# Raw weights in slots of their own, pinned weight splitting and paired down projections in a two-layer decoder step

## The chip, the cores and the metric

The kernel runs on one NeuronCore of one Trainium2 chip. The metric is the time of one execution on the device in microseconds (us). An execution's "span" is the time from its first to its last instruction; its own time is a little longer.

## The reference, cut to what matters

The program is one inference step of a decoder with two layers for 512 new prompt tokens and 8 x 4 sample tokens, which share all weights; here they are one block of 544 token columns. Each layer has a first FFN, a mixing stage (windowed attention, a causal depthwise convolution, gates, three output projections) and a second FFN, with a layer norm after each.

```python
def swiglu(x, w_up, w_down):
    a, u = jnp.split(x @ w_up, 2, axis=-1)
    return (jax.nn.silu(a) * u) @ w_down

def decoder_layer(x, k_past, v_past, conv_past, p):
    x = layer_norm(ALPHA * x + 0.5 * swiglu(x, p['ffn1_up'], p['ffn1_down']), p['ln1_g'], p['ln1_b'])
    ...
    x = layer_norm(ALPHA * x + mix @ p['w_out'], p['ln2_g'], p['ln2_b'])
    x = layer_norm(ALPHA * x + 0.5 * swiglu(x, p['ffn2_up'], p['ffn2_down']), p['ln3_g'], p['ln3_b'])
```

All data is float32. The model width is 1024, the FFN's hidden width 2816.

## The kernel before

**Arithmetic.** Activations lie transposed: 1024 features are four tiles ("pairs") of 128 partitions x 2 x 544 tokens. A product keeps float32 accuracy on a faster matrix type by splitting each operand into a high part (a cast on ScalarE) and a low part (the difference, on VectorE) and adding three matmuls: high x high, high x low, low x high. So every weight is loaded raw by SyncE's queue, cast (`halves`, L265) and subtracted (L266) before TensorE can use it, and every activation is split the same way (`split`, L346 and L347).

**Pieces.** `plan` (L155) writes down the order of all weight pieces. `fetch` (L242) loads the next one, `prep` (L269) splits it, `W` (L315) hands it out and keeps a given number of pieces prepared ahead. A normal piece is 8 x 128 rows by 256 columns, two raw tiles of 512 KB. `unit` (L324) multiplies one piece with one half of the tokens ("hf", 272 columns each): 6 matmuls for each 128 rows.

**The FFN.** The hidden width is 11 blocks of 256 columns. In the first FFN of layer 0 each block takes an "a" and a "u" piece: `silu`, then `gated`. The other three calls, here called fast, do so for blocks 0 and 1 (`up_first`, L512, half by half) and for block 10; blocks 2 to 9 go as "s" pieces of 128 columns each, where seven products of 12 matmuls replace eight (Strassen's scheme in Winograd's form, over the column halves a and u, row halves and token halves). `combine` (L282) builds the sums of raw weights on VectorE (L290 to L293) and splits four tiles. `up_fast` (L555) runs the products in the order 1, 7, (3 of the unit before, in `finish`), 6, 4, 2, 5; between them copies out of PSUM stand on ScalarE (L564, L566, L569), additions on VectorE, a silu. I call this a block unit.

**Down projections.** Blocks are grouped in threes (`GROUPS = (3, 3, 3, 2)`). After the first block of a group the down projection of the group before runs: four pieces, each with both token halves (`down_unit`, L578), whose result is added to Y in SBUF (L581, called the eviction). The last group's down projection, with block 10 just before it, is interleaved with the layer norm in `tail` (L644) or, in the last call, `final` (L667). The norm of one half (`ln_fin`, L356) is put off into the matmuls of the next half by a clock that counts matmuls (`due`, L624); its steps give X of the next stage.

**What sets the order.** The program is written in one order, and a list scheduler with a model of the engines orders each engine's instructions from it and places the buffers. An instruction passed to `keep_in_program_order` is pinned behind the one traced before it on its engine. Before the change little is pinned. Buffers come from pools of equal slots: `pp` (39 slots of a pair's size: activations, raw weights and their halves alike), `fp` (10 small slots), PSUM `ps2` (3) and `ps1` (2). A load waits on SyncE's queue until its slot is free.

**Mix.** `mix` (L843) runs projections, attention, the sample tokens' attention and the convolution (taps on VectorE, L934; sample windows on GpSimd, L949) interleaved; the convolution's state is loaded on SyncE into small slots (L879). `kf` (last keys), `uo` and `vx` (values) have buffers of their own here.

## Time and profile before

| | us |
|---|---|
| three runs | 2704.52, 2696.23, 2702.84 |
| median | 2702.84 |
| the profiled execution | 2699.76 |
| its span | 2697.8 |
| granted TensorE clock, mean over the span | 0.975 |

The stages by TensorE's work: first FFN of layer 0 to 422 us, mix to 948, fast FFN to 1349, fast FFN to 1757, mix to 2277, fast FFN to the end at 2697.8.

How to read the profile: PE is TensorE's matmul, PEld its weight load, DVE VectorE, ACT ScalarE, POOL GpSimd, SP SyncE with the DMA queue; a "q" behind the name is the engine's sequencer. L537 is line 537 of the kernel. A row of a group reads: line, engine, operation, output<-inputs, shapes, xcount | busy us, mean ns of one | idle time before them and who ended it. A row of the timeline reads: start us, duration us, engine, line, operation, and in brackets the idle time before it. A row of waits reads: who <- for whom: us in total, times, longest. In the rows, "pa" and "pb" are PSUM tiles, "pr" pairs, "wh" and "wl" the high and low halves of weights, "f" small buffers.

### The profile page before, as it was taken

Reading aid. Unit: us, or ns where it says so; the run is one execution under the profiler, and the core shown is the slowest. Engines: PE = TensorE matmul, PEld = TensorE weight load, DVE = VectorE, ACT = ScalarE, POOL = GpSimd, SP = SyncE. Lnnn points to the kernel's source line nnn. Section 1 sums busy time; section 2 is a strip of 40 time slices with the busy share of each in tenths; the row PEclk is TensorE's granted clock in tenths of the full one; section 3 lists DMA queues with packets and bytes.
Section 4 is the critical chain, followed back from the end, with each engine's and each line's share of the span. In section 5 each row is a group of like instructions: output and inputs, shape, how many; then the busy total and the mean of one; then the engine's idle time right before and its main releaser. Section 6 shows DMA issues by size and latency. Waiting matters only on the chain.

```text
span 2697.8 us, 47547 instructions
## 1 busy us (share of the span) xinstructions
PE 2568.8 (95%) x20110; PEld 2515.7 (93%) x20110; DVE 1695.7 (63%) x2555; ACT 1115.0 (41%) x1946; POOL 269.7 (10%) x532
## 2 busy tenths in 40 slices
PE   8999999989899999999989999999898999999997
PEld 7999999978899989999989999999798999999997
DVE  4324246896985575756465756459969756756645
ACT  4222215566525253434253434245773443434331
POOL 2000001422300000000010000013232000000001
PEclk9999999999999999999999999999999999999999
DMA  6223123121332213323222323222214232232341
GB/s 203 80 90 102 53 92 97 51 75 59 81 96 71 90 52 94 90 87 114 95 85 90 88 90 118 80 77 68 67 52 106 71 99 75 63 94 83 91 141 34
DMA packets 302789, 232.16 MB, mean 86 GB/s; under 512 B 43976, under 2 KB 300180, under 8 KB 302480
## 3 DMA queue, kind: packets, MB, share of 16 engines
q1 hardware_dynamic: 298768, 220.37, 27.4%
q0 software_dynamic: 3808, 8.76, 1.0%
q8 instruction: 158, 2.59, 0.4%
q14 instruction: 55, 0.45, 0.1%
HBM read 225.69 MB, written 9.16 MB: 87 GB/s over the span
## 4 chain that ended last, share of the span: by engine, by line
PE 78%; DVE 9%; ACT 6%; DMA 3%; POOL 2%; issue 2%; SPq 0%; DVEq 0%; POOLq 0%; ACTq 0%
PE pa L337 20%; PE pa L339 20%; PE pa L338 19%; PE pa L537 8%; PE pb L537 6%; DMA raw<-in_ffn_up_dram 3%; DVE pr L934 3%; DVE wl L266 2%; POOL f L949 2%; ACT wh L265 2%; ACT pr L346 1%; PE pa L1044 1%; DVE pr L347 1%; PE pb L1073 1%; DVE raw L291 0%
## 5 line engine op out<-in xcount | busy, mean ns | idle before, releaser
L337 PE MATMUL pa<-pr,wh 128*128 128x272 f32 (+2 forms) x4800 | 1402.0, 293 | 31.7 <-DVE sm L1054 13.1
L339 PE MATMUL pa<-pr,wl 128*128 128x272 f32 (+2 forms) x4800 | 1397.1, 292 | 19.0 <-DVE wl L266 19.0
L338 PE MATMUL pa<-pr,wh 128*128 128x272 f32 (+2 forms) x4800 | 1392.4, 290 | 5.9 <-DVE pr L347 5.9
L337 PEld LDWEIGHTS pa<-pr,wh 128*128 128x128 f32 x4800 | 912.3, 190 | 39.1 <-DVE sm L1054 14.0
L339 PEld LDWEIGHTS pa<-pr,wl 128*128 128x128 f32 x4800 | 912.5, 190 | 23.1 <-DVE wl L266 21.2
L338 PEld LDWEIGHTS pa<-pr,wh 128*128 128x128 f32 x4800 | 919.1, 191 | 8.7 <-DVE pr L347 7.5
L265 ACT CAST wh<-raw 128x1024 fp32r<-128x1024 f32 (+1 forms) x424 | 413.1, 999 | 379.7 <-DMA raw<-in_ffn_up_dram 109.1
L266 DVE TENSOR_TENSOR wl<-raw,wh 128x1024 fp32r<-128x1024 f32 (+1 forms) x424 | 488.8, 1164 | 114.5 <-ACT wh L265 69.6
L934 DVE SCALAR_TENSOR_TENSOR pr<-u,cw,pr 128x512 f32<-128x512 f32 x480 | 343.9, 771 | 2.2 <-ACT pr L927 2.2
L537 PE MATMUL pa<-pr,wh 128*128 128x272 f32 x1536 | 304.5, 295 | 29.2 <-ACT f L566 21.5
L537 PEld LDWEIGHTS pa<-pr,wh 128*128 128x128 f32 x1536 | 245.6, 192 | 35.7 <-ACT f L566 25.7
L537 PE MATMUL pa<-pr,wl 128*128 128x272 f32 x768 | 225.2, 293 | 7.3 <-DVE wl L266 7.3
L581 DVE SCALAR_TENSOR_TENSOR pr<-pa,pr 128x544 f32<-128x544 f32 (+2 forms) x128 | 92.1, 722 | 182.0 <-PE pa L339 181.8
L416 POOL TENSOR_SCALAR nw<-nw 91x3 f32<-91x3 f32 (+2 forms) x16 | 6.4, 401 | 1741.3 <-DVE nw L412 1741.3
L346 ACT CAST pr<-f 128x544 fp32r<-128x544 f32 (+1 forms) x122 | 78.5, 648 | 202.9 <-DVE f L489 134.0
L537 PEld LDWEIGHTS pa<-pr,wl 128*128 128x128 f32 x768 | 147.8, 192 | 8.4 <-DVE wl L266 8.4
L537 PE MATMUL pb<-pr,wh 128*128 128x272 f32 x768 | 153.9, 292 | 0.0
L489 DVE TENSOR_TENSOR f<-pa,f 128x544 f32<-128x544 f32 (+2 forms) x40 | 28.9, 722 | 170.3 <-PE pa L339 156.3
L537 PEld LDWEIGHTS pb<-pr,wh 128*128 128x128 f32 x768 | 123.7, 192 | 0.0
L537 PE MATMUL pb<-pr,wl 128*128 128x272 f32 x384 | 111.5, 292 | 0.0
L347 DVE TENSOR_TENSOR pr<-f,pr 128x544 fp32r<-128x544 f32 (+1 forms) x122 | 87.6, 720 | 24.4 <-ACT pr L346 23.9
L949 POOL TENSOR_TENSOR f<-f,cw 128x124 f32<-128x124 f32 x128 | 97.2, 797 | 12.9 <-ACT f L888 12.6
(213 smaller groups left out, 2313.5 us busy)
## 6 DMA issues: line engine op xcount, KB each, us to landing
raw<-in_ffn_up_dram SPq DMA_DIRECT2D x174, 512.0 KB, 4.5
raw<-in_w_in_dram SPq DMA_DIRECT2D x72, 512.0 KB, 3.7
raw<-in_ffn_down_dram SPq DMA_DIRECT2D x64, 512.0 KB, 3.4
raw<-in_ffn_down_dram SPq DMA_DIRECT2D x48, 256.0 KB, 3.4
raw<-in_w_in_dram SPq DMA_DIRECT2D x64, 128.0 KB, 3.0
raw<-in_w_attn_out_dram SPq DMA_DIRECT2D x32, 256.0 KB, 4.2
raw<-in_w_conv_out_dram SPq DMA_DIRECT2D x16, 512.0 KB, 3.5
raw<-in_w_out_dram SPq DMA_DIRECT2D x16, 512.0 KB, 3.5
```

The lines of the kernel that those rows point to most:

```text
L265: ins = self.nc.scalar.copy(wh, t)
L266: self.nc.vector.tensor_tensor(wl, t, wh.bitcast(F32), op=ALU.subtract)
L337: self.nc.tensor.matmul(o, lhsT=wh, rhs=h, start=k == 0, stop=False)
L338: self.nc.tensor.matmul(o, lhsT=wh, rhs=lo, start=False, stop=False)
L339: self.nc.tensor.matmul(o, lhsT=wl, rhs=h, start=False, stop=k == kk - 1)
L346: pin(self.nc.scalar.copy(hi, src))
L347: pin(self.nc.vector.tensor_tensor(lo, src, hi.bitcast(F32), op=ALU.subtract))
L489: nc.vector.tensor_tensor(sa, ps, sa, op=ALU.mult)
L537: mm = lambda a, b, first=False, last=False: nc.tensor.matmul(o, lhsT=a, rhs=b, start=first, stop=last, skip_group_check=True)
L581: nc.vector.scalar_tensor_tensor(Y[p][:, :, hs], ps, 0.5, Y[p][:, :, hs], op0=ALU.mult, op1=ALU.add)
L934: self.last["cw"] = nc.vector.scalar_tensor_tensor(cc[:, m, 0:SEQ], u[:, m, k:k + SEQ], cw[:, 8 * k + c:8 * k + c + 1], cc[:, m, 0:SEQ], o ...
L949: nc.gpsimd.tensor_tensor(pr[:, 4 * b:4 * b + 4, :], win, wv.unsqueeze(1).to_broadcast([128, DS, KC]), op=ALU.mult)
```

## The change

- Raw weights get a pool of their own, `wp`, five slots; the shared pool shrinks from 39 to 37.
- In the fast calls, `steps` cuts the splitting of a piece into steps, each with a cost for ScalarE and VectorE and the slots it takes. `fill`, called at the end of each product and down unit, emits steps as long as the accounts `ta` and `td` stay within 0.4 us of TensorE's `tp` and slots (`room`) are left. Every ScalarE and VectorE instruction of this part is pinned. `V` hands out a piece and emits its missing steps at once if there are any.
- The weight sums are rebuilt in place of the raw tile, with as many operations as before. With "hi" for a cast and "lo" for a low half, the eight steps of a block piece are: hi a and S3 = a11-a21; a21 += a22; hi z (of S3) and lo a; hi u and a11 = a21-a11; a12 -= a11; hi s (the raw a tile, rewritten) and lo z; lo u; lo s.
- The seven products of a unit run in the order 1, 7, 6, 2, 5, 4, 3, and none is left for the next unit; its gate (`rest`) is emitted ahead of the next unit.
- Down projections go by two blocks (`GROUPF = (2, 2, 2, 2, 2, 1)`), in pairs of pieces between block units (`fast_order`); block 10's a piece, with its first half, comes ahead of the down projection of group 4, outside the planned steps (`P`, which pins the casts and prepares two pieces ahead), and only block 10 is left for the last group.
- `kf`, `uo` and the sample values move to small slots, the prompt values to a pair slot; the constant `c_sel` is loaded per layer into a small slot.

```diff
+GROUPF = (2, 2, 2, 2, 2, 1)
-LA, LAU, LAV, LAS, TAP, LAG, FPB = 2, 3, 2, 2, 1.2, 0.0, 10
+LA, LAU, LAV, TAP, LAG, FPB, WPB = 2, 3, 2, 1.2, 0.0, 10, 5
-PPB = 39
+PPB = 37
+ROOM = 11
+SLACK = 0.4
+        self.wp = pool("wp", WPB)
...
+    def fast_order():
+        o = [("a", 0), ("u", 0), ("a", 1), ("u", 1)]
+        o += [("dn", 0, p, hf) for hf in range(2) for p in range(2)]
+        s = lambda j, m: ("s", 2 * j + m)
+        d = lambda g, p: [("dn", g, p, hf) for hf in range(2)]
+        o += [s(2, 0), *d(0, 2), s(2, 1), *d(0, 3), s(3, 0), s(3, 1)]
+        for g in range(1, 4):
+            j = 2 * g + 2
+            o += [s(j, 0), *d(g, 0), *d(g, 1), s(j, 1), *d(g, 2), *d(g, 3), s(j + 1, 0), s(j + 1, 1)]
+        o += [("a", 10), *d(4, 0), *d(4, 1), *d(4, 2), *d(4, 3), ("u", 10)]
+        return o + [("dn", 5, p, 0) for p in range(4)]
...
-            t = self.pp.tile([128, n, 256] if kk else [128, 8, 128], F32, tag="pair", name=self.nm("raw"))
+            t = self.wp.tile([128, n, 256] if kk else [128, 8, 128], F32, tag="raw", name=self.nm("raw"))
...
+    def steps(self, key, kk, raw):
...
+        if kk:
+            for k, t in enumerate(raw):
+                w = t.shape[1] / 4
+                out.append((1.0 * w, 0, 2, lambda k=k, t=t: hi(f"d{k}", t)))
+                out.append((0, 1.2 * w, 0, lambda k=k, t=t: lo(f"d{k}", t)))
...
+        out = [(1.05, 0.7, 2, s1),
+               (0, 0.7, 0, lambda: pin(v.tensor_tensor(a21, a21, a22, op=ALU.add))),
+               (0.6, 1.2, 0, s3),
+               (1.05, 0.7, 2, s4),
+               (0, 0.7, 0, lambda: sub(a12, a12, a11)),
+               (1.05, 0.7, 2, s6),
+               (0, 1.2, 0, lambda: lo("u", Lu)),
+               (0, 1.2, 0, lambda: lo("s", La))]
...
+    def more(self):
+        n = len({c[0] for c in self.todo})
+        while n < 3 and self.loaded < self.stop:
+            got = self.fetch()
+            out, done = self.steps(*got)
...
+    def fill(self):
+        self.more()
+        end = self.tp + SLACK
+        self.ta, self.td = max(self.ta, self.tp - 3), max(self.td, self.tp - 3)
+        while self.todo:
+            _, ca, cd, room, _, _ = self.todo[0]
+            if self.ta + ca > end or self.td + cd > end or room > self.room:
+                break
+            self.step()
+
+    def V(self, *key):
+        self.more()
+        while not self.ready:
+            self.step()
...
+    def P(self, *key):
+        self.ahead(2)
+        return self.W(*key, la=1)
...
+            self.tp += 1.5
+            self.room += room
+            self.fill()
...
             product(1, b1, w, True)
-            nc.scalar.copy(A, b1)
+            pin(act.copy(A, b1))
             product(7, E, w, True)
-            nc.scalar.copy(pu[:, 1], E)
-            finish()
+            pin(act.copy(pu[:, 1], E))
             product(6, A, w)
...
+            product(3, A, w, room=2)
+            pin(act.activation(sa[:, 1], A, AF.Silu))
...
+            def rest():
+                pin(v.tensor_tensor(sa, sa, pu, op=ALU.mult))
+                self.split(hh[:, m].rearrange("p (h n) -> p h n", h=2), hl[:, m].rearrange("p (h n) -> p h n", h=2),
+                           sa, pin)
...
+        def middle():
+            self.stop = self.pi + len(self.ffn_order(l, f)) - 14
+            self.room = ROOM
+            self.tp, self.ta, self.td = 0.0, 0.0, 4.0
...
+                    w = self.V(l, f, "s", k[0])[0]
...
+                    if rest:
+                        rest()
+                    rest = up_fast(j // 2, w, hs[j], m)
...
+            rest()
+
+        if self.is_fast(l, f):
+            gl, jl = len(GROUPF) - 1, 10
+            up_first()
+            Y += self.scaled(Y0)
+            self.mark(l, f)
+            middle()
+            wa = self.P(l, f, "a", 10)
+            if last:
+                self.cut = FB[FK[1][0]][0]
+            sa0 = silu(wa, 0)
+            down(gl - 1, self.P)
...
-        kf = self.cp.tile([128, 2, NT - CUT], F32, tag="kf", name=self.nm("kf"))
+        kf = self.f1([128, 2, NT - CUT])
-        uo = self.cp.tile([128, 8, KC - 1 + NS], F32, tag="uo", name=self.nm("uo"))
+        uo = self.f1([128, 8, KC - 1 + NS])
-        vx = self.cp.tile([128, 5, NKV, HD], F32, tag="vx", name=self.nm("vx"))
+        vp = self.att([128, 4, NKV, HD])
+        vs = self.f1([NS, NKV, HD])
```

More of the change, by code (lines that the diff above doesn't have):

```diff
@@ L270, in prep @@
         key, kk, raw = got or self.fetch()
-        if not kk:
-            self.ready.append((key, self.combine(*raw), kk))
-            return
+        assert kk
         ms = []
@@ L280, in prep, with hi, lo @@
         self.ready.append((key, ms, kk))
-    def combine(self, La, Lu):
-        v = self.nc.vector
-        Ls = self.pp.tile([128, 2, 4, 128], F32, tag="pair", name=self.nm("ls"))
-        L4 = self.f1([128, 4, 128])
+    def steps(self, key, kk, raw):
+        pin = self.tc.keep_in_program_order
+        v, act = self.nc.vector, self.nc.scalar
+        new = lambda shape, n: self.pp.tile(shape, F32R, tag="pair", name=self.nm(n))
+        sub = lambda o, a, b: pin(v.tensor_tensor(o, a, b, op=ALU.subtract))
+        low = lambda o, t, h: sub(o, t, h.bitcast(F32))
+        box = {}
+        out = []
+        def hi(n, t):
+            shape = list(t.shape)
+            small = shape[1] * shape[2] <= 512 and n == "z"
+            mk = (lambda: self.f1(shape, F32R)) if small else (lambda: new(shape, "w" + n))
+            box[n] = mk(), mk()
+            pin(act.copy(box[n][0], t))
+        def lo(n, t):
+            low(box[n][1], t, box[n][0])
+        if kk:
[3 more added lines that the diff above has]
+                out.append((0, 1.2 * w, 0, lambda k=k, t=t: lo(f"d{k}", t)))
+            return out, lambda: self.ready.append((key, [box[f"d{k}"] for k in range(len(raw))], kk))
+        La, Lu = raw
@@ L296, in combine, with s1 @@
[L296 to L301 removed]
+        S3 = self.f1([128, 4, 128])
+        def s1():
+            hi("a", La)
+            sub(S3, a11, a21)
@@ new lines, in done @@
+        def done():
+            both = lambda t, cut: tuple(cut(x) for x in t)
+            a, s, u = box["a"], box["s"], box["u"]
+            self.ready.append((key, {
+                1: both(a, lambda x: blk(x, 0)), 2: both(a, lambda x: blk(x, 1)), 7: box["z"],
+                6: both(s, lambda x: blk(x, 0)), 3: both(s, lambda x: blk(x, 1)),
+                5: both(u, lambda x: blk(x, 0)), 4: both(u, lambda x: blk(x, 1))}, kk))
+        return out, done
+    def more(self):
[3 more added lines that the diff above has]
+            out, done = self.steps(*got)
+            for i, c in enumerate(out):
+                self.todo.append((got[0], *c, done if i == len(out) - 1 else None))
+            n += 1
@@ new lines, in step @@
+    def step(self):
+        _, ca, cd, room, fn, done = self.todo.popleft()
+        self.ta += ca
+        self.td += cd
+        self.room -= room
+        fn()
+        if done:
+            done()
+        self.more()
[8 more added lines that the diff above has]
+            self.step()
@@ L588, in down @@
             del H[g]
-        for g, n in enumerate(GROUPS):
-            if g == 0:
-                up_first()
-                Y += self.scaled(Y0) if Y0 else self.residual(X)
-                if f == "ffn1":
-                    if l == 0:
-                        self.setup2()
-                    self.setup_layer(l)
-            if g == 1 and f == "ffn1":
-                self.shift_caches(l)
-            for i in range(2 if g == 0 else 0, n - (g == 3)):
-                up(g, i)
-                if i == 0 and g > 0:
-                    down(g - 1)
@@ new lines, in ffn @@
+        if self.is_fast(l, f):
+            gl, jl = len(GROUPF) - 1, 10
[8 more added lines that the diff above has]
+            down(gl - 1, self.P)
+        else:
+            gl, jl, sa0 = len(GROUPS) - 1, 10, None
+            for g, n in enumerate(GROUPS):
+                if g == 0:
+                    up_first()
+                    Y += self.residual(X)
+                    self.mark(l, f)
+                if g == 1:
+                    self.shift_caches(l)
+                for i in range(2 if g == 0 else 0, n - (g == 3)):
+                    up(g, i)
+                    if i == 0 and g > 0:
+                        down(g - 1)
+            wa = self.W(l, f, "a", 10)
@@ L608, in ffn @@
+        wu = self.P(l, f, "u", 10) if self.is_fast(l, f) else self.W(l, f, "u", 10, la=1)
+        h = new_h(gl)
         ws = []
         def pre(hf):
-            sa = silu(wa, hf)
+            sa = silu(wa, hf) if hf or sa0 is None else sa0
             if hf == 0:
                 self.ahead(A2)
-                ws.extend(self.W(l, f, "dn", 3, p, la=1) for p in range(4))
+                ws.extend(self.W(l, f, "dn", gl, p, la=1) for p in range(4))
             gated(wu, h, hf, sa)
@@ L819, in setup_layer @@
         ps = self.p1()
-        nc.tensor.matmul(ps[:, :4], lhsT=self.sel, rhs=sk4[:4], start=True, stop=True)
+        sel = self.f1([4, 128])
+        nc.gpsimd.dma_start(sel, a["c_sel"])
+        nc.tensor.matmul(ps[:, :4], lhsT=sel, rhs=sk4[:4], start=True, stop=True)
         nc.vector.tensor_copy(nsks, ps[:, :4])
```

136 lines of the change are left out of this document (78 added, 58 removed).

## The prediction

> **What bounds the kernel now.** I read the page first, then busy time by stage, the waits, and the chain.
>
> ```profile
> span 2697.8 us, 47547 instructions
> ...
> PE 2568.8 (95%) x20110; PEld 2515.7 (93%) x20110; DVE 1695.7 (63%) x2555; ACT 1115.0 (41%) x1946; POOL 269.7 (10%) x532
> ```
>
> TensorE is the bound. The diff adds and removes no matmul: the same pieces are multiplied in another order. So everything it can win or lose is time in which TensorE stands or runs slowly. The profiled execution took 2699.76 us, of which 2697.8 are the span; the median of the three runs, 2702.84, lies 3.1 above it. I make the sum against 2699.76 and put the forecast on the median, with those 3.1 added.
>
> How fast can TensorE go? The chain has runs of unhindered products:
>
> ```profile
> 1103.30 3.03 PE pa L537 x24
> 1106.33 3.00 PE pb L537 x24
> ```
>
> 48 matmuls in 6.03 us: 0.1257 us each, so a product of 12 takes 1.51 and a down unit of 24 takes 3.02. With that pitch the stages can be weighed. Columns: stretch, length, PE busy (instructions), PEld, DVE, ACT, POOL, granted clock, DMA share, GB/s.
>
> ```profile
> 422.00:948.00 526.00, 499.14 (x3916) 479.37 (x3915) 391.63 (x663) 258.86 (x515) 104.45 (x192) 0.96 0.27 77
> 1002.30:1300.90 298.60, 286.12 (x2226) 283.58 (x2225) 184.96 (x244) 114.55 (x186) 0.00 (x0) 0.98 0.32 96
> 1409.60:1708.00 298.40, 286.91 (x2228) 284.12 (x2229) 184.05 (x246) 113.59 (x185) 0.00 (x0) 0.98 0.33 96
> 2330.10:2627.80 297.70, 284.70 (x2225) 281.94 (x2224) 184.71 (x244) 114.30 (x186) 1.20 (x2) 0.99 0.33 99
> ```
>
> The last three are the block units of the three fast FFN calls. At 0.1257 their matmuls need 279.8, 280.1 and 279.7 us, so 18.8, 18.3 and 18.0 us are lost: 55.1 in all. That is the most the rewritten part can win, 2% of the span. The first row is a mix stage; the change touches it only through its buffers. Where in the block units is the loss?
>
> ```profile
> 1002.30:1022.40 20.10, 14.62 (x78) 13.63 (x77) 17.26 (x22) 8.83 (x13) 0.00 (x0) 0.75 0.19 53
> 1022.40:1250.00 227.60, 220.60 (x1744) 219.05 (x1744) 146.12 (x196) 92.49 (x155) 0.00 (x0) 1.00 0.31 91
> 1250.00:1300.90 50.90, 50.90 (x408) 50.90 (x407) 21.58 (x28) 13.23 (x19) 0.00 (x0) 1.00 0.42 135
> 1409.60:1446.40 36.80, 32.33 (x215) 31.09 (x216) 27.85 (x40) 15.95 (x26) 0.00 (x0) 0.81 0.21 58
> 2330.10:2367.00 36.90, 31.39 (x222) 30.16 (x220) 28.94 (x38) 16.99 (x28) 0.00 (x0) 0.91 0.21 59
> ```
>
> The start of each call (rows 1, 4, 5) loses 20.1-9.8 = 10.3, 36.8-27.0 = 9.8 and 36.9-27.9 = 9.0: 29.1. The steady part (row 2) loses 227.6-219.2 = 8.4; by difference the other two calls lose 8.5 and 9.0, so 26.0. The end (row 3: 408 matmuls need 51.3) loses nothing. These are the three terms to follow.
>
> **The start.** Its loss is a wait and what it does to the clock: first the waiting matmul, then the clock.
>
> ```profile
> 1005.79 0.59 PE L537 MATMUL pa<-pr,wl 128*128 128x272 f32 x1 [2.90 <-DVE wl L266]
> ```
>
> ```profile
> 1005.20:1012.00 6.80, 5.75 (x24) 5.43 (x25) 5.71 (x8) 3.84 (x5) 0.00 (x0) 0.50 0.00 0
> 1018.90:1022.30 3.40, 3.40 (x17) 3.40 (x16) 2.50 (x4) 0.19 (x1) 0.00 (x0) 0.51 0.02 5
> ```
>
> After 2.90 us of waiting the granted clock is 0.50 for 6.8 us (lost: half, 3.4); a later stall costs another 3.4 us at 0.51 (lost 1.7). I call these a long and a short spell. [...]
>
> What VectorE did just before shows the sizes: a gate's product, two subtractions of weights, a low half.
>
> ```profile
> 1002.55 0.72 DVE L489 TENSOR_TENSOR f<-pa,f 128x544 f32<-128x544 f32 x1 [4.08 <-PE pa L339]
> 1003.19 0.68 DVE L290 TENSOR_TENSOR ls<-raw,raw 128x512 f32<-128x512 f32 x1
> 1003.91 0.69 DVE L291 TENSOR_TENSOR raw<-raw 128x512 f32<-128x512 f32 x1
> 1004.52 1.22 DVE L266 TENSOR_TENSOR wl<-raw,wh 128x1024 fp32r<-128x1024 f32 x1
> ```
>
> And ScalarE, from a stretch that the steady part needs again: silu, casts of weights, cast of the hidden value, copies out of PSUM.
>
> ```profile
> 1119.02 0.40 ACT L551 ACTIVATE f<-pb 128x272 f32<-128x272 f32 x1 [1.08 <-PE pb L537]
> 1119.31 1.04 ACT L265 CAST wh<-ls 128x1024 fp32r<-128x1024 f32 x1
> 1120.25 0.62 ACT L265 CAST f<-f 128x512 fp32r<-128x512 f32 x1
> 1120.77 1.05 ACT L265 CAST wh<-raw 128x1024 fp32r<-128x1024 f32 x1
> 1121.72 0.64 ACT L346 CAST pr<-f 128x544 fp32r<-128x544 f32 x1
> 1122.26 0.39 ACT L566 COPY f<-pa 128x272 f32<-128x272 f32 x1
> 1122.54 0.40 ACT L569 COPY f<-pb 128x272 f32<-128x272 f32 x1
> 1122.82 0.41 ACT L564 COPY pb<-pa 128x272 f32<-128x272 f32 x1
> ```
>
> After the change the first work is a down unit. Its casts are early, but its low half is pinned on VectorE behind the last gate of the opening blocks: product 0.72, cast of the hidden value 0.64 on ScalarE, its low half, as wide as the product, 0.72, then the weight's low half 1.22. That is 3.3 us after TensorE has finished; two matmuls run before the low half is needed, so 3.1 are idle, as long as the 2.90 of before, and I give it the same 3.4 of clock. The splits of the first block piece are pinned behind the eviction of the fourth down unit: 0.72 for a tile of that width, then one addition 0.69 and the low half 1.22, less the two free matmuls 2.4; then two subtractions and a half-size low half (0.68+0.69+0.68) behind product 1 and two matmuls (1.76): 0.3; then two low halves (2.44) behind one product (1.51): 0.9. With a short spell, 1.7, the start is 3.1+3.4+2.4+0.3+0.9+1.7 = 11.8, three times 35.4 against 29.1: **+6**. The second down piece's low half is pinned behind the first unit's eviction; TensorE, whose order is free, can run the first piece's second half meanwhile, and if it doesn't, 0.72+1.22 = 1.9 more stand open. In the second call the layer's constants are traced in between, and I take the same. Bounds: without any slow clock 6.7 each, 20.1, or -9; with long spells for both stalls and the 1.9, 15.4 each, 46.2, or +17.
>
> **The steady part.** In the eight rows above is the stall of today, which recurs every two block units: L566, a copy that empties PSUM for the next product, stands behind four casts, and TensorE waits until it is done. The pinned steps cure this inside a unit: they are set between the products by an account kept in the code, in which no step may end more than 0.4 us after the product it is set behind, and each copy has a product of 1.51 as its cover. But where two block units follow each other without a down unit, the written order is: cast of a later weight 1.05 (it takes the slot that product 3 frees, so it starts only then, and the silu and all of ScalarE queue behind it), in the worse case its low half on VectorE 1.22, then the gate's product 0.72, its cast 0.64, and only then the copy that product 6 of the next unit waits for, 0.41: 4.0 us against products 1 and 7, 3.0. About 1.0 us at six such places a call is 6. TensorE's own order is not pinned and may put a product of a later unit there, so 0 is the other bound. I take 5, nearer to today's 8.4, which has the same freedom: 3 x 5 against 26.0, **-11** (-8 to -26).
>
> The counts cost nothing by themselves. A block piece is split with four additions or subtractions, four casts and four low halves, as before. The down groups of two blocks add 16 evictions a call, 3 x 16 x 0.72 = 34.6 us of VectorE, hidden while VectorE works 185 of 298.6 us; without that cover they would cost that much. Loads:
>
> ```profile
> raw<-in_ffn_up_dram SPq DMA_DIRECT2D x174, 512.0 KB, 4.5
> ```
>
> Five raw slots hold two block pieces and a half; the next piece is fetched a unit (10.6 us) ahead of a landing of 4.5, so ScalarE's pinned casts should not meet a missing load. The extra load of c_sel on GpSimd's queue is needed by no one before mix.
>
> **The end.** This is new. Piece ("a", 10) leaves the planned steps; its cast is pinned on ScalarE behind the last block's rest. From the last product: silu 0.40, product 0.72, cast of h 0.64, cast of the weight 1.05, its low half 1.22, less two matmuls: 3.8 us idle, with nothing else for TensorE, where row 3 above lost none. It is longer than the 2.90, so a short spell or a long one: 1.7 to 3.4, I take 2.5. 6.3, three times: **+19** (11 with no slow clock, 22 with long spells).
>
> **The tail.** The last down group shrinks from two blocks to one, and half of block 10 moves ahead. Between the last eviction of the first half and its normalised X, today:
>
> ```profile
> 1325.31 0.72 DVE L581 SCALAR_TENSOR_TENSOR pr<-pa,pr 128x544 f32<-128x544 f32 x1 [1.51 <-PE pa L339]
> ...
> 1354.51 0.72 DVE L347 TENSOR_TENSOR pr<-pr,pr 128x544 fp32r<-128x544 f32 x1
> ```
>
> ```profile
> 1355.29 0.60 PE L338 MATMUL pa<-pr,wh 128*128 128x272 f32 x1 [2.01 <-DVE pr L347]
> ```
>
> 29.2 us of normalisation have 192 matmuls, 24.1 us, beside them, and TensorE waits at the end. After the change 144 matmuls, 18.1, are left. If the normalisation gains nothing, 6 more us are open; if its steps, which are set by TensorE's progress, move up as much, 0. I take 3, at two such ends: **+6**. The final call has no stage behind it.
>
> **Mix.** SyncE waits for buffers:
>
> ```profile
> SPq L162 <- PE pa L339: 658.3, 100, 29.2
> ...
> SPq L879 <- DVE pr L952: 34.8, 2, 17.8
> ```
>
> ```profile
> PE pa L339 <- DVE wl L266: 19.0, 10, 5.9
> ```
>
> Raw weights no longer wait for a slot of the shared pool (first row), so part of the 19.0 us in which low halves come late should go, with the slow clock behind it. Against that, three long-lived tiles (kf, uo, the sample values) move into the ten small buffers, for which the state loads of L879 wait already, and these stand in the same queue ahead of weights. I take **-8** for both stages together; bounds -28 (19.0 plus three spells of 3.4 of clock) and +20 (the longest wait of L879, 17.8, once more in one stage).
>
> Sum: 6-11+19+6-8 = +12; 2699.8+12 = 2711.8 on the profiled execution, 2715 on the median.
>
> **Rivals.** (1) *Faster: slots were the disease.* If late raw weights cause most waits, mix gives back 28 instead of 8 and the steady part 26 instead of 11: 12-20-15 = -23, 2680. For it: the 658.3 us of slot waits on SyncE. Against it: today's repeating gap ends with ScalarE's order (the eight rows), not with a load. It decides from 20 us beyond what I took, 12 to undo the sum and 8 to be measurable. 0.35 for all that ends faster. [...] (2) *Nothing measurable:* the stalls at the ends are half as dear (no slow clock, normalisation moves up): 12-7-6 = -1, 2702. 0.20. (3) *Much slower:* the small buffers choke mix, +20 instead of -8: 2743. For it: L879. Against it: those tiles can be loaded late. 0.12.
>
> **The numbers.** A measurement of this kernel can tell 0.3%, 8 us. My forecast, +8 to +30 with its middle at 2715, has 0.33 and its own range 2711 to 2733; with rival 3, slower has 0.45, same 0.20, faster 0.35. The range reaches from a little beyond rival 1 to rival 3: 2676 to 2742.
>
> **What would show it.** Right: the start of each call still at half clock, about 12 us lost; a wait of about 3.8 us on L265/L266 where block 10 begins, absent today; copies no longer behind casts inside a unit; the wait on the split X longer by about 3. Wrong: a start without a wait of 3 us, or block 10 beginning at once (then faster); or mix, 526 us today, moved by more than 10 us either way.

## The result, and the profile after

| | before | after |
|---|---|---|
| runs, us | 2704.52, 2696.23, 2702.84, 2700.74 | 2779.95, 2781.07, 2782.53 |
| median of these, us | 2701.79 | 2781.07 |
| the profiled execution, us | 2699.76 | 2779.95 |
| granted TensorE clock, mean | 0.975 | 0.968 |

The changed kernel is slower: 1.0297 times the time before, 95% interval 1.0275 to 1.0318. A fourth execution after the change, 3590.61 us at a granted clock of 0.648, is left out of the ratio. The forecast was 2715, in a range of 2676 to 2742: slower was right, the size was not.

The page of the changed kernel, its head and the row of busy time:

```profile
span 2778.2 us, 47552 instructions
...
PE 2603.3 (94%) x20110; PEld 2540.0 (91%) x20110; DVE 1725.8 (62%) x2591; ACT 1126.9 (41%) x1938; POOL 301.7 (11%) x533
```

The matmuls are as many as before (x20110). So I count the 80.4 us by which the span grew (2778.2 less 2697.8) as time in which TensorE stands or runs at a lower granted clock: 0.968 in the mean where it was 0.975, and 0.50 to 0.51 in stretches that the last section shows. To place them I cut each execution at the first matmul of the layer norm that ends each stage and count, in each stretch, its length less 0.1257 us for each matmul in it; I call this the loss. A loss by counts is safer than the length of a stage, because the mark may move past some matmuls. Columns: stretch, length, PE busy (matmuls), PEld, DVE, ACT, POOL, granted clock, DMA share, GB/s. The stages are mix, fast FFN, fast FFN, mix, fast FFN. Before:

```profile
404.50:930.30 525.80, 498.94 (x3915) 479.17 (x3914) 394.02 (x664) 263.45 (x520) 106.25 (x193) 0.96 0.26 76
930.30:1329.90 399.60, 384.30 (x3002) 380.72 (x3002) 245.55 (x333) 158.53 (x249) 6.63 (x22) 0.99 0.29 88
1329.90:1737.00 407.10, 389.70 (x3026) 385.90 (x3026) 250.64 (x342) 160.05 (x252) 16.95 (x42) 0.97 0.31 94
1737.00:2257.90 520.90, 497.33 (x3914) 477.10 (x3913) 393.93 (x664) 263.10 (x520) 107.66 (x192) 0.97 0.26 77
2257.90:2697.80 439.90, 406.99 (x3196) 402.82 (x3194) 267.41 (x371) 164.72 (x261) 15.94 (x46) 0.98 0.28 85
```

After:

```profile
404.90:917.90 513.00, 492.65 (x3894) 472.54 (x3893) 393.97 (x663) 262.30 (x520) 125.89 (x193) 0.98 0.28 80
917.90:1351.80 433.90, 403.46 (x3073) 397.24 (x3072) 255.59 (x346) 160.79 (x245) 4.27 (x22) 0.97 0.26 78
1351.80:1787.50 435.70, 399.92 (x3026) 393.45 (x3026) 259.94 (x354) 162.75 (x248) 18.30 (x43) 0.96 0.28 88
1787.50:2302.10 514.60, 490.89 (x3844) 469.48 (x3843) 394.47 (x663) 268.04 (x524) 123.87 (x192) 0.97 0.27 80
2302.10:2778.20 476.10, 424.96 (x3216) 417.55 (x3214) 277.67 (x384) 167.62 (x257) 13.06 (x46) 0.95 0.24 73
```

Losses before: 33.7, 22.2, 26.7, 28.9, 38.2. After: 23.5, 47.6, 55.3, 31.4, 71.8. The two mix stages lose 62.6 before and 54.9 after, 7.7 less; the three fast calls 87.1 and 174.8, 87.7 more. Inside the first of these calls, in order: the start of the block units, the steady part, the beginning of block 10, the tail.

```profile
975.00:1020.00 45.00, 39.58 (x286) 38.79 (x285) 24.16 (x33) 15.60 (x19) 0.00 (x0) 0.91 0.11 33
1020.00:1290.00 270.00, 253.67 (x1963) 250.64 (x1962) 167.47 (x222) 104.31 (x165) 0.00 (x0) 0.98 0.29 89
1290.00:1305.30 15.30, 11.99 (x73) 11.45 (x73) 5.83 (x7) 4.67 (x7) 0.00 (x0) 0.78 0.24 74
1305.30:1420.00 114.70, 103.95 (x801) 102.07 (x800) 69.27 (x101) 42.95 (x62) 18.30 (x43) 0.97 0.31 100
```

Losses: 9.0, 23.3, 6.1, 14.0. The steady part, which lost 8.4 before, is the largest. It loses at three places that come back every 72 to 74 us, that is once in four block units and eight down units. Here are two of them, in rows of the timeline (start, duration, engine, line, operation, idle time before). First, ScalarE, VectorE and TensorE around a copy out of PSUM:

```profile
1138.44 0.40 ACT L678 ACTIVATE f<-pb 128x272 f32<-128x272 f32 x1 [0.37 <-PE pb L647]
1140.46 0.64 ACT L462 CAST pr<-f 128x544 fp32r<-128x544 f32 x1 [1.62 <-DVE f L684]
1141.02 0.38 ACT L666 COPY pb<-pa 128x272 f32<-128x272 f32 x1
```

```profile
1138.38 0.68 DVE L312 TENSOR_TENSOR raw<-raw,raw 128x512 f32<-128x512 f32 x1
1139.10 0.69 DVE L312 TENSOR_TENSOR raw<-raw 128x512 f32<-128x512 f32 x1
1139.71 0.72 DVE L684 TENSOR_TENSOR f<-f,f 128x544 f32<-128x544 f32 x1
```

```profile
1141.45 1.77 PE L647 MATMUL pa<-pr,f 128*128 128x272 f32 x12 [1.63 <-ACT pb L666]
```

The silu of one unit is done at 1138.84. VectorE has two subtractions of weights pinned ahead of the gate's product (L684); ScalarE waits 1.62 us for that product with its cast (L462), and the next unit's copy (L666) is pinned behind this cast. TensorE waits for the copy. The matmuls that wait are those of product 7: their weights "f" are the split of S3, the only weights in a small buffer. The rows show that the copy was held by the cast and not by its input: TensorE had finished product 1, the copy's input, by 1139.8, and the copy starts only at 1141.02, when the cast (1140.46, 0.64 us) is all but done.

Second, an eviction behind the same gate chain:

```profile
1165.48 1.22 DVE L312 TENSOR_TENSOR wu<-raw,wu 128x1024 fp32r<-128x1024 f32 x1
1166.62 1.22 DVE L312 TENSOR_TENSOR ws<-raw,ws 128x1024 fp32r<-128x1024 f32 x1
1167.75 0.72 DVE L684 TENSOR_TENSOR f<-f,f 128x544 f32<-128x544 f32 x1
1169.18 0.73 DVE L463 TENSOR_TENSOR pr<-f,pr 128x544 fp32r<-128x544 f32 x1 [0.71 <-ACT pr L462]
1169.83 1.35 DVE L694 SCALAR_TENSOR_TENSOR pr<-pa,pr 128x544 f32<-128x544 f32 x2
```

```profile
1159.49 0.28 PE L455 MATMUL pa<-pr,wd 128*128 128x272 f32 x1
...
1168.63 0.29 PE L455 MATMUL pa<-pr,wd 128*128 128x272 f32 x1
1170.69 0.36 PE L453 MATMUL pa<-pr,wd 128*128 128x272 f32 x1 [1.77 <-DVE pr L694]
```

The two evictions (L694, x2) are ten us late. The scheduler, free to order TensorE's work, had put two down units between the products of the block unit, and TensorE finished them by 1159.8 (first row); a third followed the unit's last product and took the last of the three tiles of its PSUM pool, and at 1168.9 there was none for the fourth. But VectorE's evictions are pinned behind the unit's gate chain, which needs the last product (done at 1165.9), and behind two low halves of weights; the chain's own low half waited 0.71 us more for ScalarE. The third place is the single matmul that is written ahead of product 1 (L663, here called the dummy): it waits 1.1 us for a cast of weights on ScalarE and stands in the list of waits at run 5, below. Behind some of these waits TensorE also runs at half clock (0.50 and 0.51) for 3.4 us; the last section has the rows.

At the start, and where block 10 begins:

```profile
998.08 0.55 PE L453 MATMUL pa<-pr,wd 128*128 128x272 f32 x1 [2.26 <-ACT wd L322]
1014.36 0.39 PE L647 MATMUL pa<-pr,wa 128*128 128x272 f32 x1 [2.30 <-DVE wa L312]
1298.85 0.60 PE L453 MATMUL pa<-pr,wh 128*128 128x272 f32 x1 [2.87 <-ACT wh L291]
```

### The profile page after: what moved, and what is told of

It is laid out like the page before. It is cut to its first block, busy times and chain, and to the rows that moved or that the text cites. A ratio compares the mean times of both kernels' runs of the same rounds, so it can differ in the third digit from the quotient of the medians.

```text
span 2778.2 us, 47552 instructions
## 1 busy us (share of the span) xinstructions
PE 2603.3 (94%) x20110; PEld 2540.0 (91%) x20110; DVE 1725.8 (62%) x2591; ACT 1126.9 (41%) x1938; POOL 301.7 (11%) x533
## 4 chain that ended last, share of the span: by engine, by line
PE 71%; DVE 14%; POOL 7%; ACT 4%; issue 3%; DMA 1%; DVEq 0%; POOLq 0%; ACTq 0%
PE pa L455 17%; PE pa L453 17%; PE pa L454 17%; PE pa L647 9%; PE pb L647 7%; POOL f L1110 3%; DVE pr L1095 3%; POOL pr L1114 2%; DVE wl L292 1%; ACT pr L462 1%; DVE raw L312 1%; DVE pr L463 1%; DVE f L684 1%; DVE ws L312 1%; DVE pr L694 1%
## 5 line engine op out<-in xcount | busy, mean ns | idle before, releaser
L453 PE MATMUL pa<-pr,wh 128*128 128x272 f32 (+1 forms) x4032 | 1181.2, 295 | 39.2 <-ACT pr L462 22.5
L455 PE MATMUL pa<-pr,wl 128*128 128x272 f32 (+1 forms) x4032 | 1178.1, 293 | 18.1 <-DVE wl L292 17.7
L454 PE MATMUL pa<-pr,wh 128*128 128x272 f32 (+1 forms) x4032 | 1177.2, 293 | 4.6 <-DVE pr L463 3.9
L453 PEld LDWEIGHTS pa<-pr,wh 128*128 128x128 f32 x4032 | 769.5, 192 | 48.1 <-ACT pr L462 25.7
L455 PEld LDWEIGHTS pa<-pr,wl 128*128 128x128 f32 x4032 | 771.3, 192 | 20.4 <-DVE wl L292 20.1
L454 PEld LDWEIGHTS pa<-pr,wh 128*128 128x128 f32 x4032 | 776.4, 193 | 10.0 <-DVE pr L463 8.0
L292 DVE TENSOR_TENSOR wl<-raw,wh 128x1024 fp32r<-128x1024 f32 (+1 forms) x268 | 309.5, 1182 | 89.5 <-ACT wh L291 58.8
L453 PE MATMUL pa<-pr,wd 128*128 128x272 f32 x768 | 226.4, 297 | 21.8 <-DVE pr L694 16.7
L454 PE MATMUL pa<-pr,wd 128*128 128x272 f32 x768 | 225.5, 294 | 0.0
L455 PE MATMUL pa<-pr,wd 128*128 128x272 f32 x768 | 224.6, 296 | 0.5 <-DVE wd L312 0.5
L694 DVE SCALAR_TENSOR_TENSOR pr<-pa,pr 128x544 f32<-128x544 f32 (+2 forms) x176 | 124.3, 720 | 126.7 <-PE pa L455 126.7
L462 ACT CAST pr<-f 128x544 fp32r<-128x544 f32 (+1 forms) x124 | 79.7, 646 | 290.0 <-DVE f L605 166.5
L453 PEld LDWEIGHTS pa<-pr,wd 128*128 128x128 f32 x768 | 149.3, 195 | 25.5 <-issue 20.6
L647 PE MATMUL pa<-pr,wa 128*128 128x272 f32 x1152 | 164.6, 292 | 6.9 <-DVE wa L312 6.9
L647 PE MATMUL pb<-pr,ws 128*128 128x272 f32 x1152 | 165.0, 294 | 0.0
L647 PEld LDWEIGHTS pb<-pr,ws 128*128 128x128 f32 x1152 | 155.5, 195 | 0.0
L454 PEld LDWEIGHTS pa<-pr,wd 128*128 128x128 f32 x768 | 150.2, 196 | 0.0
L455 PEld LDWEIGHTS pa<-pr,wd 128*128 128x128 f32 x768 | 148.7, 195 | 1.0 <-DVE wd L312 1.0
```

Source lines behind the costliest of these rows:

```text
L292: self.nc.vector.tensor_tensor(wl, t, wh.bitcast(F32), op=ALU.subtract)
L453: self.nc.tensor.matmul(o, lhsT=wh, rhs=h, start=k == 0, stop=False)
L454: self.nc.tensor.matmul(o, lhsT=wh, rhs=lo, start=False, stop=False)
L455: self.nc.tensor.matmul(o, lhsT=wl, rhs=h, start=False, stop=k == kk - 1)
L462: pin(self.nc.scalar.copy(hi, src))
L647: mm = lambda a, b, first=False, last=False: nc.tensor.matmul(o, lhsT=a, rhs=b, start=first, stop=last, skip_group_check=True)
```

## The experiments

The losses of every run, by the same count, in the two mix stages and the three fast calls. Ratios are to the kernel before, measured beside each run.

| run | median us | ratio, 95% | mix | fast calls |
|---|---|---|---|---|
| before | 2701.79 | | 62.6 | 87.1 |
| after | 2781.07 | 1.0297 (1.0275 to 1.0318) | 54.9 | 174.8 |
| 1 before, storage of the change | 2653.73 | 0.9841 (0.9824 to 0.9857) | 47.8 | 54.8 |
| 2 before, 41 common slots | 2690.45 | 0.9970 (0.9958 to 0.9982) | 64.6 | 75.6 |
| 3 before, four raw slots | 2654.28 | 0.9838 (0.9823 to 0.9852) | 46.8 | 55.8 |
| 4 after, no pins in the middle | 2686.61 | 0.9958 (0.9943 to 0.9973) | 56.2 | 78.0 |
| 5 after, evictions free | 2734.89 | 1.0140 (1.0124 to 1.0155) | 55.5 | 127.0 |
| 6 after, weight steps free | 2753.44 | 1.0209 (1.0192 to 1.0226) | 56.6 | 145.2 |
| 7 after, only weight steps pinned | 2706.99 | 1.0028 (1.0016 to 1.0041) | 58.1 | 101.3 |
| 8 after, block 10 by steps | 2753.93 | 1.0209 (1.0194 to 1.0224) | 56.3 | 149.4 |
| 9 runs 4 and 8 together | 2673.82 | 0.9907 (0.9892 to 0.9922) | 56.1 | 66.9 |
| 10 run 9, last group of two | 2639.59 | 0.9784 (0.9769 to 0.9798) | 51.0 | 37.3 |
| 11 after, order mended, pinned | 2763.38 | 1.0244 (1.0228 to 1.0259) | 54.1 | 159.1 |
| 12 run 10, order mended, pinned | 2724.57 | 1.0101 (1.0086 to 1.0116) | 47.5 | 129.4 |

The theory after the result: the storage gives time back, the written and pinned order of ScalarE and VectorE takes more than that, and the ends of a call add to it. The rival: the order of the units itself costs the time, pinned or not.

### Storage: runs 1 to 3

Run 1 is the kernel before with the change's buffers alone.

```diff
-PPB = 39
+PPB = 37
...
+        self.wp = pool("wp", WPB)
...
-            t = self.pp.tile([128, n, 256] if kk else [128, 8, 128], F32, tag="pair", name=self.nm("raw"))
+            t = self.wp.tile([128, n, 256] if kk else [128, 8, 128], F32, tag="raw", name=self.nm("raw"))
...
```

> The kernel before with only the storage of the change: raw weights in five slots of their own, 37 pair slots instead of 39, the four small tensors moved to the shared small slots; order, casts and block units as before. Theory (the gain of 18 to 19 us in the two mix stages comes from the raw slots, since prefetch there no longer waits for a pair slot; the loss of some 98 us lies in the new order and its pins): about 2684 us, faster than before by 15 to 20 us, the mix stages about 515 us each between the marks of the layer norms. Rival (the mix gain comes from the new order in the calls on either side): 2702 us within 5, mix stages 526 and 521 us as before. Second rival (two fewer pair slots starve the old order of the block units): slower than 2710 us.

Measured: 2653.73, more than expected. Mix gives back 14.8, and the fast calls, of which the expectation had said nothing, give back 32.3. Is it the number of slots or their being apart? Run 2 has run 1's moved small tensors and 41 common slots; run 3 is run 1 with four raw slots, so 41 in all.

```diff
-PPB = 39
+PPB = 41
...
```

> The kernel before with the small tensors moved as in the change, and the freed storage put into more of the common slots (41 instead of 39) in place of five slots for raw weights alone. Theory (what the raw slots give is that a raw transfer never waits for a slot of long life to come free): 2690 to 2702 us, well above the 2654 of the kernel with slots of its own for raw weights. Rival (what counts is the number of slots): within 8 us of 2654.

```diff
-LA, LAU, LAV, LAS, TAP, LAG, FPB, WPB = 2, 3, 2, 2, 1.2, 0.0, 10, 5
+LA, LAU, LAV, LAS, TAP, LAG, FPB, WPB = 2, 3, 2, 2, 1.2, 0.0, 10, 4
```

> The kernel before with the small tensors moved and four slots for raw weights beside 37 pair slots, 41 in all: as many as the run that kept 41 common slots (2690 us), one fewer than the run with five raw slots (2654). Theory (raw weights need slots that no long-lived tile takes, not more slots): 2655 to 2670 us. Rival (the number of slots decides): 2685 to 2695.

Measured: 2690.45 and 2654.28. Equal in number, 36 us apart: raw weights need slots that no long-lived tile can take. The waits of TensorE for the copy of L566, the repeating gap of the prediction, show what that buys. Before, and in run 2:

```profile
PE pa L537 <- ACT f L566: 21.5, 19, 1.9
```

```profile
PE pa L537 <- ACT f L566: 12.0, 13, 1.9
```

In runs 1 and 3 no matmul waits for this copy. The waits of ScalarE's casts for a transfer fall in the same order, before, in run 2, in run 3:

```profile
ACT wh L265 <- DMA raw<-in_ffn_up_dram: 109.1, 38, 7.1
```

```profile
ACT wh L265 <- DMA raw<-in_ffn_up_dram: 74.9, 32, 6.7
```

```profile
ACT wh L266 <- DMA raw<-in_ffn_up_dram: 42.8, 30, 4.5
```

So late loads and late copies go together. The step between is argued and not shown: a cast that waits for its transfer would hold up the copies behind it on ScalarE, but in the eight rows of the prediction the casts ahead of the copy stand back to back, and none of them waits for a transfer. The scheduler's order on ScalarE also differs between the kernel before and run 1, and no run separates that from the loads. Run 1's fast call between 1014.2 and the layer norm has no stop of TensorE over 0.5 us.

### Pins: runs 4 to 7

Run 4 takes every pin of the middle (the part of a fast call from the first down unit to the last block unit) away and leaves the written order.

```diff
     def steps(self, key, kk, raw):
-        pin = self.tc.keep_in_program_order
+        pin = lambda i: i
...
     def ffn(self, l, f, XYT, vg, vb, last):
-        pin = self.tc.keep_in_program_order
+        pin = lambda i: i
```

> The changed kernel with none of the pins of the middle: steps, copies, adds, gate chain and evictions are written in the same order but the scheduler may place them. Theory (the loss comes from instructions held in the written order on ScalarE and VectorE, not from the order of units): 2710 to 2740 us. Rival (the loss comes from the order of the units, with down pairs between block units and one block in the last group): 2775 to 2790 us. Second rival (the pins keep casts from going ahead of copies, and without them copies wait longer as in the kernel before): slower than 2800 us.

Measured: 2686.61, faster than the theory's 2710 to 2740. The loss of the fast calls falls by 96.8 to 78.0, and the steady part is clean:

```profile
1020.00:1260.00 240.00, 239.51 (x1909) 239.07 (x1908) 159.00 (x213) 98.56 (x159) 0.00 (x0) 1.00 0.32 95
```

1909 matmuls need 240.0 us: nothing is lost, with the same units, the same 16 extra evictions a call and the same casts. The rival, the order of the units as written, falls. TensorE's own order changed with the pins, since the scheduler sets it: in run 4 product 1 of two units, at 1111.38 and 1113.01, stands ahead of product 7 of the first. So the run prices the pins together with the order that they leave to TensorE. Which pins? Run 5 frees the evictions alone, run 6 the weight steps alone, run 7 all but the weight steps.

```diff
-                    down_unit(D[g, p], g, p, hf, pin)
+                    down_unit(D[g, p], g, p, hf)
```

> The changed kernel with one thing undone: the evictions of the down units in the middle of a fast call are no longer pinned in the order written, so they need not stand behind the gate chain on VectorE. Theory (the evictions behind the gate chain hold the PSUM slots of the down units and stop TensorE for 1.9 us once per four block units, some ten times over the three calls): 2782 falls by 15 to 22 us, to 2760 to 2767, and the idle time of L453 and L647 that ends on L694 shrinks to a few us. Rival (the stall is the copies behind casts on ScalarE, and an unpinned eviction only lets the next wait appear there): 2776 to 2784, with the idle time on L666 growing by what L694 loses.

Measured: a gain of 46 us, twice what the theory gave. The waits of TensorE of the changed kernel that stand in a steady part, and what run 5 leaves of them:

```profile
PE pa L647 <- ACT pb L666: 23.6, 15, 2.2
...
PE pa L453 <- DVE pr L694: 16.7, 14, 1.8
...
PE pb L663 <- ACT wa L322: 10.1, 9, 1.1
```

```profile
PE pa L647 <- ACT pb L666: 23.6, 15, 2.2
```

Two of the three recurring waits go, not one: the dummy's wait on the cast is gone with the eviction's. Time at half clock goes with them. The steady part of the first call now runs at a granted clock of 1.00 and loses 8.9 us, where it lost 23.3 at 0.98:

```profile
1020.00:1275.00 255.00, 247.83 (x1958) 246.47 (x1958) 167.50 (x222) 103.76 (x165) 0.00 (x0) 1.00 0.32 94
```

Of these 14.4 us, the waits that are gone make 9.2 (5.8 for evictions, 3.4 for the cast) and two spells of half clock 3.4.

```diff
     def steps(self, key, kk, raw):
-        pin = self.tc.keep_in_program_order
+        pin = lambda i: i
```

> The changed kernel with only the casts of the weight steps unpinned; copies, adds, gate chain and evictions of the block units and down units keep their written order among themselves. Theory (two separate causes: evictions held behind the gate chain, and copies held behind casts): the copy and dummy waits on ScalarE go (30 to 45 us), the waits on the eviction stay (about 20 us): 2735 to 2755 us. Rival (one cause, the evictions behind the chain; casts matter little): 2770 us or more. Second rival (all of the loss comes from where the casts stand): 2690 to 2710 us.

Measured: 2753, inside the first theory's numbers but not by its mechanism. The copy still waits:

```profile
PE pa L647 <- ACT pb L666: 21.8, 15, 2.2
PE pa L453 <- DVE pr L694: 19.3, 21, 1.9
```

Run 6 frees the casts of the steps and also their subtractions and low halves, so the copies are held mainly by the gate chain written ahead of them, and by no weight step. At 1133.88, for example, the gate's product follows the silu with no subtraction ahead of it, and the copy still makes TensorE wait 1.33 us.

```diff
     def ffn(self, l, f, XYT, vg, vb, last):
-        pin = self.tc.keep_in_program_order
+        pin = lambda i: i
```

> The changed kernel with the pins on the weight steps alone: copies, adds, gate chains and evictions of the middle are free, so the casts keep their order among themselves but not against the block units. Theory (a queue loses when both kinds stand in one written order; an order among the casts alone costs nothing, since they are in order anyway): 2685 to 2695 us, as with no pins at all (2687). Rival (each kind of pin has its own price, and the casts' share is the 28 us that freeing them gave): 2705 to 2730 us.

Measured: 2707, the rival's number: against run 4 the pins of the weight steps cost 20 us. They cost most of it at the start of a call. In the first fast call 45 us hold 294 matmuls from 975 to 1020, 8.0 lost, where run 4 has 358 and loses none, and the whole call loses 9.7 more than in run 4; from 1020 to 1260 only 2.4 are lost (1890 matmuls). The start waits as in the changed kernel, 2.26 us for a cast (L322) at 1002.56 and 2.30 us for a low half (L312) at 1018.89; the 2.30 stands in all three calls. Run 4 has neither wait in this call. The prices do not add up: 46 and 28 alone against 94 together, where the weight steps' share is 20 with all else free. A wait that one edit removes can uncover another: the waits for an eviction (L694), 14 in the changed kernel, are 21 in run 6.

### The ends of a call: runs 8 to 10

Run 8: block 10's first piece goes through the planned steps.

```diff
-            self.stop = self.pi + len(self.ffn_order(l, f)) - 14
+            self.stop = self.pi + len(self.ffn_order(l, f)) - 13
...
-            wa = self.P(l, f, "a", 10)
+            wa = self.V(l, f, "a", 10)
```

> The changed kernel with the first half of block 10 taken through the planned steps instead of being cast in one go behind the last block unit's rest. Theory (that cast leaves TensorE idle for 3.3 us and at half clock for 6.8 us, in each of three calls, some 6 us each): 2764 to 2768 us, and the idle time on L291 and L292 of piece a 10 gone. Rival (the same wait moves to the next piece or step, since ScalarE and VectorE are late there anyway): 2778 to 2784 us.

Measured: a gain of 27 us, more than the 17.3 that the beginning of block 10 loses in the changed kernel (6.1, 5.5 and 5.7 in the three calls). Where the other 10 come from, this run alone does not settle: its order of matmuls differs from the changed kernel's in the tail as well.

Run 9 is runs 4 and 8 together.

> The two edits that have paid together: no pins in the middle of a fast call, and the first half of block 10 taken through the planned steps. Theory (the two losses are separate: held order in the middle, and the cast of block 10 at its end): 2687 falls by three calls of 3.7 us idle and 3.4 us at half clock, some 21 us, to 2661 to 2669. Rival (without pins the scheduler already places that cast as early as it can, so nothing is left to gain): 2682 to 2690.

Measured: 2673.8, 13 under run 4: between theory and rival. Of the wait at the beginning of block 10, 1.6 to 1.7 us are left in each call.

Run 10 turns the groups of the down projection round, one block first and two last. It also puts block 10's two pieces next to each other, and the down projection of group 4 between the block units of block 9.

```diff
-GROUPF = (2, 2, 2, 2, 2, 1)
+GROUPF = (1, 2, 2, 2, 2, 2)
...
-            j = 2 * g + 2
+            j = 2 * g + 1
...
-        o += [("a", 10), *d(4, 0), *d(4, 1), *d(4, 2), *d(4, 3), ("u", 10)]
+        o += [s(9, 0), *d(4, 0), *d(4, 1), s(9, 1), *d(4, 2), *d(4, 3), ("a", 10), ("u", 10)]
```

> The kernel of the run before (no pins, block 10 through the steps) with the groups of the down projection turned round: the first group has one block and the last has two, as many pieces and evictions as before. Theory (in the tail a last group of one block makes each down unit wait for the split that has just been made, 1.5 to 3.4 us at five places, since no other block's products can go first; two blocks hide it): 8 to 15 us faster than the run before it, 2648 to 2658 if that one gives 2665, and the idle time on the hidden split line falls under 10 us. Rival (the waits in the tail are those of the layer norm's chain on GpSimd and stay): within 4 us of the run before it.

Measured: a gain of 34 us, more than twice the theory, and the fastest kernel of the study: 2639.59, 0.9784 of the time before. In the final call, run 9 waits for the split of a hidden value just made:

```profile
2643.81 0.58 PE L453 MATMUL pa<-pr,wh 128*128 128x256 f32 x1 [3.36 <-ACT pr L462]
```

Run 10 has no such wait there. With two blocks in the last group there are products of the other block that can run first and cover silu, gate and split. The losses of the three fast calls fall from 10.6, 18.9 and 37.4 to 5.8, 8.8 and 22.6.

### Pins in a better order: runs 11 and 12

Run 11 keeps every pin of the changed kernel and moves three things in the written order: `then` is written ahead of a product's weight steps, `fill=False` leaves the steps out, and `first` is the copy and behind it the gate chain of the unit before.

```diff
-            product(1, b1, w, True)
-            pin(act.copy(A, b1))
+            product(1, b1, w, True, then=first)
...
-            product(3, A, w, room=2)
-            pin(act.activation(sa[:, 1], A, AF.Silu))
+            product(3, A, w, room=2, then=lambda: pin(act.activation(sa[:, 1], A, AF.Silu)), fill=False)
```

> The changed kernel with every pin kept and three places of the written order changed: a product's copy, add or silu is written ahead of the weight steps that follow it; no weight steps are written between a block unit's last silu and its gate chain; and where two block units follow each other, the gate chain is written behind the next unit's first copy. Theory (the pins cost because of the order that was written, two subtractions ahead of the gate and the hidden split ahead of the copy, not as such): the 1.6 us waits on the copy, the 1.8 us waits on the eviction and the 1.1 us waits of the dummy go, some 55 us: 2720 to 2740 us. Rival (any fixed order of these queues loses, since durations and landings differ from the planned account): 2765 us or more. Second rival (the steps only slide to the next product and push the copy there): 2745 to 2765.

The same 74 us of the steady part, one period of the changed kernel, in it and in run 11:

```profile
1169.00:1243.00 74.00, 67.72 (x532) 66.91 (x532) 46.62 (x63) 29.59 (x47) 0.00 (x0) 1.00 0.31 92
```

```profile
1169.00:1243.00 74.00, 71.63 (x554) 69.65 (x553) 47.88 (x64) 30.58 (x48) 0.00 (x0) 1.00 0.29 86
```

74 - 66.9 = 7.1 lost become 74 - 69.6 = 4.4. The waits of 1.6 and 1.8 us are gone and more, shorter ones have come, of up to 0.5 us, such as this:

```profile
1170.96 0.36 PE L453 MATMUL pa<-pr,wd 128*128 128x272 f32 x1 [0.39 <-DVE pr L699]
```

The run gains 18 us in all: the second rival's number, the waits move on.

> The fastest kernel so far (no pins, block 10 through the steps, two blocks in the last group of the down projection, 2639.6 us) with the pins back, in the mended order of the run before this one. Theory (a mended order costs what is left of the start of the block units, some 4 to 9 us in each of three calls): 2650 to 2670 us. Rival (with the right order pins are free): 2635 to 2645. Second rival (any fixed order loses): 2690 us or more.

Run 12, the same order in run 10's kernel: 2724.57, 85 above run 10. The second rival (any fixed order loses) holds for the orders tried; an order with no loss may exist and wasn't found.

## Why the prediction was wrong

The terms of the sum, on the profiled execution (the losses after less those before, from windows cut in all three calls as above):

| term | predicted | measured |
|---|---|---|
| start of the block units | +6 | -2.9 (26.2 against 29.1) |
| steady part | -11 | +46.9 (72.1 against 25.2) |
| beginning of block 10 | +19 | +17.3 (none before) |
| tail, and the opening blocks of the second fast call | +6 | +20.3 (44.4 against 24.1) |
| mix | -8 | -7.7 |
| opening blocks of the other two | not in the sum | +5.3 |
| sum | +12 | +79.2 of 80.4 |

**The step that failed is the steady part.** The prediction took 5 us a call after the change; the calls lose 23.3, 24.0 and 24.9. Two sentences of it were wrong.

The first is "each copy has a product of 1.51 as its cover", with the account's 0.4 us. The account counts engine time, and not the time in which silu, gate, cast and copy wait for one another across two engines. And the cover was counted too long: the prediction let product 6 wait for the copy, behind products 1 and 7, 3.0 us. In the row of 1141.45 it is product 7 that waits, so product 1 alone runs beside the chain, which ended 1.63 us late. By run 6 the two subtractions written ahead of the gate are a small part of it: with the weight steps free, 21.8 of the 23.6 us are left. The prediction had named this place, with 1.0 us at six places a call, of which it took 5 us; measured are 15 waits of 23.6 us in three calls, 8 a call, so this part alone would have moved the forecast by some 9 us.

The other sentence is "The counts cost nothing by themselves", with the 16 evictions a call "hidden". As work they are hidden: run 4 makes all of them and loses nothing in the steady part shown. As pinned instructions they are not: each stands behind the gate chain and holds a PSUM tile while it waits. For the steady part the prediction asked only what stood ahead of a copy, and not what was pinned behind the gate on VectorE. It also put no clock loss into this term. Run 5 prices the pinned evictions, with the time at half clock that goes with them, at 46 us; the term was wrong by 58.

**The tail** was the second error, 14 us. The final call makes 10.7 of the 20.3: it lost 27.0 against 16.3. The prediction sized the norm's chain at two boundaries and excused the final call because no stage stands behind it. But with one block in the last group its down units wait for that block's own gate and split, in the final call 1.55 us at 2724.03 and 3.36 us at 2749.95, where the kernel before has no such wait. Run 10 removes both, and 34 us with them, though it changes the place of block 10's pieces too.

**What was right.** The beginning of block 10: 3.8 us of waiting were forecast, 2.87 and 0.44 measured, with 6.8 us at 0.50 of the clock behind it. The start has its two waits, 2.26 and 2.30 where 3.1 and 2.4 were forecast, but by these windows it costs 2.9 less than before and not 6 more. The wait for the split X grew by about 3, as forecast, at the first boundary (5.34 at 1374.67 against 2.01), and not at the second, where the longest is 1.21.

Mix, -7.7 where -8 was forecast, is in good part luck. It is the sum of a gain of 10.2 in the first stage and a loss of 2.5 in the second; run 1 loses 24.1 in the second, as against 31.4, so that loss is not the storage's. The first stage's length, 525.8 before and 513.0 after, moved by more than the 10 us that the prediction had named as a sign of being wrong. And the waits for late low halves, which were to give the gain, fell only from 17.6 to 15.0 us in the two stages together.

**Rival 1 had the right cause and the wrong company.** "Slots were the disease" had been set aside because the repeating gap ended on ScalarE's order and not on a load. Runs 1 to 3 show that the gap goes with the raw weights' slots: 21.5 us of waits for the copy before, 12.0 with as many common slots, none with slots of their own. Storage alone gives 1.6%, 47 us of loss in the five stages, and the forecast had -8 for it in mix and nothing of its own in the calls, where 32 lay. The order and its pins then took 120 (174.8 against run 1's 54.8). In the changed kernel a PSUM tile was missing too, and run 5 shows that a late eviction held it; a larger PSUM pool was not tried.

Not settled: why run 8 gains 10 us more than the beginning of block 10 had lost, and which part of run 10's 34 us comes from the new places of block 10's pieces and of group 4's down projection rather than from the group's size.

## What to carry to other kernels

Here a pin kept a copy behind a cast that waited 1.62 us, and two evictions until ten us after the matmuls whose tiles they empty: before fixing the order of an engine's instructions, list for each one that frees a PSUM tile what stands in front of it, what that waits for, and which matmul waits behind it, latency included, since an account of busy time cannot see it. A wait that ends on an engine's order can still go with late loads, as the waits for the copy did here (21.5 us before, none in runs 1 and 3), so follow it one step further before ruling storage out. When a change has parts, price each alone: here storage gave 1.6% and hid inside a result 3% slower.

## What the runs showed of the hardware

The operands split into high and low parts ran on a faster type: in the kernel before, a matmul record of 128x272 on unsplit float32 (L368) took 392 ns on average, one on split operands (L337 to L339) 290 to 293.

The length of a short wait did not decide here whether it cost clock. In the first fast call of the changed kernel the wait of 1.77 us for an eviction comes three times, ending at 1096.74, 1170.69 and 1243.09. Behind the first and the third the granted clock is 0.51 and 0.50 for 3.4 us, behind the second it is 1.00:

```profile
1097.10:1100.50 3.40, 3.40 (x18) 3.40 (x17) 1.89 (x3) 0.00 (x0) 0.00 (x0) 0.51 0.38 112
1170.70:1174.10 3.40, 3.40 (x27) 3.40 (x28) 2.37 (x4) 0.34 (x1) 0.00 (x0) 1.00 0.36 98
1243.90:1247.30 3.40, 3.40 (x17) 3.40 (x16) 1.44 (x2) 0.00 (x0) 0.00 (x0) 0.50 0.45 131
```

Such a spell cost here about as much as the wait itself: from the first wait to the second it is 73.95 us, from the second to the third 72.40, with 532 matmuls in each. The waits between 1169 and 1243, of up to 1.77 us, left the clock at 1.00. A longer wait, 2.87 us at 1298.85 with 0.44 more at 1300.11, has 6.8 us at 0.50 behind it, 3.4 us lost:

```profile
1298.50:1305.30 6.80, 6.02 (x25) 5.70 (x26) 3.60 (x4) 2.19 (x3) 0.00 (x0) 0.50 0.52 165
```

What decides which of the short waits is followed by half clock, these runs do not show.
